# A two-layer decoder trunk: two single products of the attention branch become one seven-product pair

## The chip, the cores and the metric

The kernel runs on one core of a Trainium2 chip. The metric is the device time of one execution in microseconds (us). The time of the kernel before is 2420.99 us, the median of three runs (2418.62 to 2423.28).

## What is computed

The trunk has two layers over 256 positions of width 2048, in fp32. The part that matters here:

```python
for l in range(DEPTH):                                   # 2 layers
    h = rms_norm(x, mix_norm[l])
    q, k, v, uv, gate_logits = split(h @ w_in[l])        # 2048 x 7680
    branch_a = sliding_window_attention(q, k, v, sinks[l]) @ w_attn_branch[l]   # 1024 x 2048
    branch_b = chunked_sgu(gelu(uv), ...) @ w_sgu_branch[l]                      # 1024 x 2048
    gates = sigmoid(gate_logits)                         # two gates per channel
    merged = gates[..., :2048] * branch_a + gates[..., 2048:] * branch_b
    x = x + merged @ w_out[l]
    h2 = rms_norm(x, ffn_norm[l])
    x = x + (silu(h2 @ w_gate[l]) * (h2 @ w_up[l])) @ w_down[l]
```

The change touches one product only, `branch_a`: the attention output (256 x 1024) times `w_attn_branch[l]` (1024 x 2048).

## The kernel before

**Chunks and halves.** Each weight matrix is cut into chunks of 512 columns, and each chunk into "halves" of 256 rows, held as a tile of 128 partitions x 2 x 512. A half comes from HBM as one load of 512 KB (for `w_attn_branch` as two loads of 256 KB each, 64 partitions apiece, `rows_of`, L129). The 256 positions are two row tiles of 128.

**Three matmuls for one.** To keep fp32 accuracy every operand is split into a high part and a rest (`hi` and `lo` for weights, `uh` and `ul` for activations). For a weight half, ScalarE (ACT) writes `whi` (L261) and VectorE (DVE) writes `wlo` = raw - whi (L262). `add_product` (L353) then issues six matmuls of 128x512: for each of the two 128-row blocks uh*hi, uh*lo, ul*hi. These six are called *one product* here. The tiles `whi` and `wlo` have four buffers, so that the split of one entry cannot start before the matmuls of the entry four places earlier are done.

**Single and pair.** `single` (L125) multiplies one chunk: each half is one entry with two products, one for each row tile. `pair` (L137) takes two chunks with the same activations. For one unit (512 rows of each chunk, four halves k11, k12, k21, k22) it uses a scheme with seven block products in place of eight (entries P1 to P7, one product each); the remaining halves are ordinary entries, G for the first chunk and U for the second. The seven products need differences of the weights, made on DVE in place in the loaded tiles (`add`, L242, L246): P5 takes k12 - k11, P6 takes k22 less that, P7 takes k22 - k12, and P4 takes k21 less what P6 took. P3 multiplies k22 itself. The sums of the activations (`sh`, `sl`) already exist for the first unit. Sums that both chunks share go through a tile `kept`: after P5, ACT copies two accumulators (L384, L385); after P6 and again after P7, DVE adds the accumulator a[1] into `kept` (L387), and since P6, P7 and P4 all accumulate in a[1], P7 must not start before the L387 that follows P6 has read it. Later ACT copies `kept` into the accumulators of the second chunk (L390).

**Order.** `plans` (L172 to L196) lists the products of a layer, and `entries` is one list of all halves in order. When a pair comes, its six head entries are woven into the last entries of the plan ahead of it (L198 to L216): with six or nine of them when that plan is long, and otherwise with four. In the variant with four entries behind a pair (L211) P6, P2 and P7 stand one behind the other. PE follows this list. The order on DVE, ACT, POOL and SP is made by a scheduler at build time.

**Loads.** All weight loads are issued on the SP queue, up to seven entries ahead (`W_LOAD`). Ordinary halves rotate through five buffers. The four tiles k11, k12, k21 and k22 have one buffer each, shared by all pairs: a pair's k22 can be loaded only when the k22 of the pair ahead has been split for its P3. The k22 load stands behind other transfers in SP's order, among them the gathers of a transpose (L437: 16 transfers of 32 KB, `tt<-box`), which wait for DVE's block transposes (L431).

**Around the change.** The attention branch comes after the projection pair of gate chunks 3 and 4, and before the projection pair of gate chunks 5 and 6. Its first two chunks are a pair already. The third and fourth were two singles of four entries each. After each chunk DVE multiplies it with the gate (`gated`, L1034, L1037).

In what follows A is the pair of attention chunks 0 and 1, B the third and fourth chunk when they are a pair, and C the projection pair of gate chunks 5 and 6. "A's U" and so on name entries of that pair.

Of the kernel before, what the change touches and what calls it, by code (L numbers as in the profile page):

```python
# [28 lines left out]
NCH = D // CW  # L29
# [34 lines left out]
def hybrid_trunk(ctx: ExitStack, tc: tile.TileContext, x, mix_norm, w_in, q_norm, k_norm, sinks,  # L64
# [31 lines left out]
    def cols_of(w_ap, n):  # L96
        return [w_ap[:, j * CW:(j + 1) * CW] for j in range(n)]
# [19 lines left out]
    def load_of(w, h, tag="raw"):  # L117
        raw_no[0] += 1
        return raw_no[0], w, h, tag

    def half(w, h, tag):
        ld = load_of(w, h)
        return dict(tag=tag, h=h, loads=[ld], src=ld[0])

    def single(key, w):  # L125

        return Plan(key, [], [half(w, h, "X") for h in range(w.shape[0] // (2 * P))])
# [9 lines left out]
    def pair(key, wa, wb, by_unit=False, last_later=False, two=False):  # L137

        head, p3 = [], []
        both = (WINO, WINO + 1) if two else (WINO,)
        for w in both:
            h1, h2 = 2 * w, 2 * w + 1
            l11, l12, l21, l22 = (load_of(m, h, t if w == WINO else "slot")
                                  for m, h, t in ((wa, h1, "k11"), (wb, h1, "k12"), (wa, h2, "k21"), (wb, h2, "k22")))
            k11, k12, k21, k22 = l11[0], l12[0], l21[0], l22[0]
            head.append([dict(tag="P1", loads=[l11, l12], src=k11),
                         dict(tag="P5", loads=[], sums=[(k11, k12, k11)], src=k11),  # L150
                         dict(tag="P2", loads=[l21, l22], src=k21),
                         dict(tag="P6", loads=[], sums=[(k11, k22, k11)], src=k11),
                         dict(tag="P7", loads=[], sums=[(k12, k22, k12)], src=k12),
                         dict(tag="P4", loads=[], sums=[(k21, k21, k11)], src=k21)])
            p3.append(dict(tag="P3", loads=[], src=k22))
            for e in head[-1] + p3[-1:]:
                e["unit"], e["done"] = w, w == both[-1]
        head = [e for es in zip(*head) for e in es]
        rest = [h for h in range(wa.shape[0] // (2 * P)) if h // 2 not in both]
        g, u = [half(wa, h, "G") for h in rest], [half(wb, h, "U") for h in rest]  # L160
        body = g[:3] + p3 + g[3:] + u
        g[1]["then"] = "open"
        if last_later:
            body = g[:2] + p3 + u[:2] + g[2:] + u[2:]
        if by_unit:
            body = g[:2] + p3 + u[:2]
            g[0]["then"] = g[1].pop("then")
            for i in range(2, len(rest), 2):
                body += g[i:i + 2] + u[i:i + 2]
        return Plan(key, head, body)  # L170

    plans, by_heads = [], []  # L172
    for l in range(DEPTH):
        wl = w_in[l]

        def of_in(kind, c):
            o = {"kv": O_KV, "q": 0, "v": O_V, "u": O_U, "gate": O_GATE}[kind] + c * CW
            return wl[:, o:o + CW]

        for f in FIRST_PART[l]:  # L180
            plans.append((single if len(f) == 1 else pair)(("in", l), *(of_in(*c) for c in f)))
        by_heads += cols_of(w_attn_branch[l], NCH)
        c_ = by_heads[-NCH:]
        plans += [pair(("att", l), c_[0], c_[1])] + [single(("att", l), w) for w in c_[2:]]
        plans[-3].first = True
        c_ = cols_of(w_sgu_branch[l], NCH)
        plans += [pair(("in", l), of_in("gate", 5), of_in("gate", 6)), pair(("sgu", l), c_[0], c_[1]),
                  single(("in", l), of_in("gate", 7)), single(("sgu", l), c_[2]), single(("sgu", l), c_[3])]
        c_ = cols_of(w_out[l], NCH)
        plans += [pair(("mix", l), c_[j], c_[j + 1], last_later=j == 0) for j in range(0, NCH, 2)]  # L190
        for r, (f0, f1) in enumerate(ROUNDS):
            for f in range(f0, f1):
                plans.append(pair(("ffn", l), w_gate[l, :, f * CW:(f + 1) * CW], w_up[l, :, f * CW:(f + 1) * CW], f == 0,
                                  two=(r, f - f0) in FFN_TWO))
            c_ = cols_of(w_down[l, f0 * CW:f1 * CW, :], NCH)
            plans += [pair(("hid", l, r), c_[j], c_[j + 1], j == 0, two=(l, r, j) in HID_TWO) for j in range(0, NCH, 2)]  # L196
# [85 lines left out]
    def tick():  # L282
        slot_no[0] += 1
        due = [s for s in steps if s[0] <= slot_no[0]]
        steps[:] = [s for s in steps if s[0] > slot_no[0]]
        for _, fn in sorted(due, key=lambda s: s[0]):
            with tc.issue_after(stream.last.ins):
                fn()
# [75 lines left out]
    def step():  # L364
        e = entries[stream.at]
        p, tag = e["plan"], e["tag"]
        units = units_at[p.key]
        w = stream.next()
        if tag in "XGU":
            ps = banks(p, "b" if tag == "U" else "a")  # L370
            todo = [(ps[t], block(units, e["h"], t)) for t in range(NT)]
        else:
            which, t, form = {"P1": ("a", 1, (0, 0)), "P2": ("a", 0, (1, 0)), "P6": ("a", 1, 1), "P7": ("a", 1, 2),
                              "P4": ("a", 1, (1, 1)), "P5": ("a", 0, 0), "P3": ("b", 0, 3)}[tag]
            todo = [(banks(p, which)[t], tuple(x[:, form] for x in units[e["unit"]][2:]) if isinstance(form, int)
                     else block(units, 2 * e["unit"] + form[0], form[1]))]
        for ps, u in todo:
            add_product(p, ps, u, w, tag in ("P4", "P7"))
        a, b = p.acc.get("a"), p.acc.get("b")
        if not e.get("done", True):  # L380
            pass
        elif tag == "P5":
            p.kept = slot([P, 2, CW], name="kept")
            nc.scalar.activation(p.kept[:, 1, :], a[0], AF.Copy)  # L384
            nc.scalar.activation(a[0], a[1], AF.Copy)  # L385
        elif tag in ("P6", "P7"):
            nc.vector.tensor_tensor(out=p.kept[:, int(tag == "P7"), :], in0=a[1], in1=p.kept[:, 1, :], op=ALU.add)  # L387
        if "then" in e:
            for t, ps in enumerate(banks(p, "b")):
                nc.scalar.activation(ps, p.kept[:, t, :], AF.Copy)  # L390
                p.opened.add(id(ps))
        p.left -= 1
        if e is getattr(p, "last_g", None):
            p.calls[0](a)
        if p.left == 0 and p.paired:
            p.calls[1](b)
        debt[0] += len(todo)
        if debt[0] >= 2:
            debt[0] -= 2
            if p.left or p.paired:  # L400
                tick()

    def run(key):
        p = plans[turn_of[0]]
        turn_of[0] += 1
        assert p.key == key
        return p

    def product(key):

        p = run(key)
        while p.left:
            step()
        return p.acc["a"]

    def product_pair(key, on_a, on_b):


        p = run(key)
        p.calls = (on_a, on_b)  # L420
        while p.left:
            step()
# [575 lines left out]
    for l in range(DEPTH):  # L998

        gates = {}  # L1000
        att, spa = Attention(layer[l]), Spatial(layer[l], norm)
# [32 lines left out]
        def gated(j, ps):  # L1034
            ga = gates[j]
            for t in range(NT):
                nc.vector.scalar_tensor_tensor(out=ga[:, t, :], in0=ga[:, t, :], scalar=1.0, in1=ps[t],  # L1037
                                               op0=ALU.add, op1=ALU.mult)

        product_pair(("att", l), lambda ps: gated(0, ps), lambda ps: gated(1, ps))  # L1040
        for j in range(2, NCH):
            gated(j, product(("att", l)))
            tick()
        mT = units_at["mix", l] = [None] * NCH
        nxt = Norm(ffn_cols(l))
        units_at["ffn", l] = nxt.units
# [93 lines left out]
```

## Time and profile before

| | |
|---|---|
| time, median of 3 runs | 2420.99 us |
| time, lowest and highest | 2418.62, 2423.28 us |
| span of the profiled execution | 2416.4 us |
| median less this span | 4.6 us |
| PE, matmuls | 2405.1 us busy, 10692 instructions |
| PEld, weight loads of PE | 1970.7 us busy, 82% of the span |
| DVE | 2092.0 us busy, 87% |
| ACT | 1532.4 us busy, 63% |
| POOL | 303.4 us busy, 13% |
| granted TensorE clock | 1.000 |

The profiled execution is known by its span alone, from its first instruction to its last; what its own run took is not listed beside it, so the span is set against the median of the other runs. Matmuls are pipelined, and their ends are modelled: a row's duration overlaps the next row's start. The stretch of attention chunks 2 and 3 lies at about 311 to 333 us in the first layer and 1512 to 1534 us in the second; times in the two layers are 1201.1 us apart.

### The profile page before, as it was taken

Reading aid. Unit: us, or ns where it says so; the run is one execution under the profiler, and the core shown is the slowest. Engines: PE = TensorE matmul, PEld = TensorE weight load, DVE = VectorE, ACT = ScalarE, POOL = GpSimd, SP = SyncE. Lnnn points to the kernel's source line nnn. Section 1 sums busy time; section 2 is a strip of 40 time slices with the busy share of each in tenths; the row PEclk is TensorE's granted clock in tenths of the full one; section 3 lists DMA queues with packets and bytes.
Section 4 is the critical chain, followed back from the end, with each engine's and each line's share of the span. In section 5 each row is a group of like instructions: output and inputs, shape, how many; then the busy total and the mean of one; then the engine's idle time right before and its main releaser. Section 6 shows DMA issues by size and latency. Waiting matters only on the chain.

```text
span 2416.4 us, 31069 instructions
## 1 busy us (share of the span) xinstructions
PE 2405.1 (100%) x10692; PEld 1970.7 (82%) x10692; DVE 2092.0 (87%) x2409; ACT 1532.4 (63%) x1932; POOL 303.4 (13%) x557
## 2 busy tenths in 40 slices
PE   9999999999999999999999999999999999999999
PEld 7877888888888888888888778888888888888887
DVE  7779787898999998799887897878889989998998
ACT  6477555576666675666665775555676666666665
POOL 1100001132110111001301000011311101110010
PEclk9999999999999999999999999999999999999999
DMA  8755678687677757776957557776867786677773
GB/s 287 233 167 164 178 204 251 221 264 239 191 238 228 239 179 223 245 225 178 293 177 260 174 160 197 215 223 227 269 219 232 213 258 204 199 231 229 235 223 138
DMA packets 285070, 527.16 MB, mean 218 GB/s; under 512 B 28208, under 2 KB 40080, under 8 KB 284912
## 3 DMA queue, kind: packets, MB, share of 16 engines
q1 hardware_dynamic: 263056, 486.36, 63.6%
q0 software_dynamic: 21536, 38.56, 6.2%
q8 instruction: 83, 1.36, 0.2%
q14 instruction: 75, 0.61, 0.1%
q10 hardware_dynamic: 320, 0.27, 0.0%
HBM read 483.66 MB, written 16.78 MB: 207 GB/s over the span
## 4 chain that ended last, share of the span: by engine, by line
PE 88%; DVE 4%; DMA 4%; issue 1%; ACT 1%; SPq 1%; POOL 0%; DVEq 0%; ACTq 0%
PE acc L361 58%; PE acc L362 29%; DVE wlo L262 2%; DMA raw<-in_w_up_dram 2%; DMA raw<-in_w_in_dram 1%; DMA tt<-box 1%; ACT whi L261 1%; DVE raw L246 1%; SPq L437 1%; PE psc L807 1%; PE po L859 0%; PE psg L942 0%; PE ppt L844 0%; PE pt L474 0%; POOL tt L437 0%
## 5 line engine op out<-in xcount | busy, mean ns | idle before, releaser
L261 ACT ACTIVATE whi<-raw 128x1024 fp32r<-128x1024 f32 (+1 forms) x1116 | 1166.6, 1058 | 786.3 <-PE acc L362 440.0
L262 DVE TENSOR_TENSOR wlo<-raw,whi 128x1024 fp32r<-128x1024 f32 (+1 forms) x1117 | 1343.5, 1216 | 269.3 <-ACT whi L261 255.3
L361 PE MATMUL acc<-whi,uh 128*128 128x512 f32 x2854 | 1116.7, 391 | 1.4 <-ACT uh L460 1.4
L361 PE MATMUL acc<-wlo,uh 128*128 128x512 f32 x2854 | 1113.3, 390 | 2.1 <-DVE wlo L262 1.3
L362 PE MATMUL acc<-whi,ul 128*128 128x512 f32 x2854 | 1112.1, 390 | 0.6 <-DVE ul L465 0.6
L361 PEld LDWEIGHTS acc<-wlo,uh 128*128 128x128 f32 x2854 | 536.0, 188 | 118.5 <-DVE wlo L262 6.6
L361 PEld LDWEIGHTS acc<-whi,uh 128*128 128x128 f32 x2854 | 535.9, 188 | 117.8 <-issue 4.9
L362 PEld LDWEIGHTS acc<-whi,ul 128*128 128x128 f32 x2854 | 535.9, 188 | 112.8 <-DVE ul L465 1.5
L437 POOL DMA_DIRECT2D tt<-box x464 | 228.0, 499 | 1202.6 <-DVE box L431 339.7
L246 DVE TENSOR_TENSOR raw<-raw,raw 128x1024 f32<-128x1024 f32 x292 | 355.5, 1218 | 5.2 <-DMA raw<-in_w_up_dram 2.9
L361 PE MATMUL acc<-wlo,sh 128*128 128x512 f32 x584 | 228.1, 391 | 2.0 <-DVE wlo L262 2.0
L361 PE MATMUL acc<-whi,sh 128*128 128x512 f32 x584 | 228.4, 391 | 0.0
L362 PE MATMUL acc<-whi,sl 128*128 128x512 f32 x584 | 227.5, 390 | 0.0
L361 PEld LDWEIGHTS acc<-wlo,sh 128*128 128x128 f32 x584 | 109.7, 188 | 26.3 <-DVE wlo L262 4.1
L361 PEld LDWEIGHTS acc<-whi,sh 128*128 128x128 f32 x584 | 109.7, 188 | 25.1 <-issue 2.3
L362 PEld LDWEIGHTS acc<-whi,sl 128*128 128x128 f32 x584 | 109.6, 188 | 22.7
L387 DVE TENSOR_TENSOR kept<-acc,kept 128x512 f32<-128x512 f32 x102 | 69.6, 682 | 9.3 <-PE acc L362 9.3
L390 ACT ACTIVATE acc<-kept 128x512 f32<-128x512 f32 x102 | 59.7, 588 | 2.3 <-DVE kept L387 1.0
L964 POOL DMA_DIRECT2D held_x<-part x16 | 13.9, 868 | 301.4 <-ACT part L963 301.4
L333 POOL TENSOR_TENSOR rv<-ve,neg_half 128x4 f32<-128x4 f32 x8 | 10.2, 1273 | 266.8 <-DVE ve L907 247.9
L384 ACT ACTIVATE kept<-acc 128x512 f32<-128x512 f32 x51 | 30.1, 591 | 10.8 <-PE acc L362 10.5
L829 ACT ACTIVATE pr<-pr,negm 128x128 f32<-128x128 f32 x64 | 24.9, 390 | 16.0 <-DVE negm L820 16.0
(149 smaller groups left out, 909.0 us busy)
## 6 DMA issues: line engine op xcount, KB each, us to landing
raw<-in_w_in_dram SPq DMA_DIRECT2D x239, 512.0 KB, 4.8
raw<-in_w_gate_dram SPq DMA_DIRECT2D x176, 512.0 KB, 4.6
raw<-in_w_up_dram SPq DMA_DIRECT2D x176, 512.0 KB, 5.4
raw<-in_w_down_dram SPq DMA_DIRECT2D x176, 512.0 KB, 5.3
raw<-in_w_out_dram SPq DMA_DIRECT2D x64, 512.0 KB, 6.9
raw<-in_w_attn_branch_dram SPq DMA_DIRECT2D x64, 256.0 KB, 7.0
raw<-in_w_sgu_branch_dram SPq DMA_DIRECT2D x32, 512.0 KB, 5.8
tt<-box POOLq DMA_DIRECT2D x464, 32.0 KB, 4.7
```

The costliest lines, as they stand in the source:

```text
L246: self.last = nc.vector.tensor_tensor(out=self.raws[d], in0=self.raws[x], in1=self.raws[y], op=ALU.subtract)
L261: self.high = nc.scalar.activation(hi[:, i, :], raw[:, i, :], AF.Copy)
L262: self.last = nc.vector.tensor_tensor(out=lo[:, i, :], in0=raw[:, i, :], in1=hi[:, i, :].bitcast(F32), op=ALU.subtract)
L361: nc.tensor.matmul(ps, a, part[:, kk, :], start=first and kk + n == 0, stop=False, skip_group_check=True)
L362: nc.tensor.matmul(ps, b, hi[:, kk, :], start=False, stop=kk == 1, skip_group_check=True)
L384: nc.scalar.activation(p.kept[:, 1, :], a[0], AF.Copy)
L387: nc.vector.tensor_tensor(out=p.kept[:, int(tag == "P7"), :], in0=a[1], in1=p.kept[:, 1, :], op=ALU.add)
L390: nc.scalar.activation(ps, p.kept[:, t, :], AF.Copy)
L437: q.dma_start(dst[j * B:(j + 1) * B, i], box[i * B:(i + 1) * B, j])
L807: nc.tensor.matmul(pscore[:, i, :nk], self.qT[pair // 4][j * HD:(j + 1) * HD, pair % 4, t * P:(t + 1) * P], self.kT[j * HD:(j + 1) * HD, : ...
L829: self.exps = nc.scalar.activation(pr4[:, h, :], pr4[:, h, :], AF.Exp, bias=nm_[:, h:h + 1], accum_out=den[:, h:h + 1])
L964: nc.gpsimd.dma_start(held_x[j], part, accum_op=ALU.add)
```

## The change

Chunks 2 and 3 of the attention branch become a second `pair` in place of two `single` plans. The mark `first` (which keeps a pair's first accumulators in the pool `ps_acc`) stays with pair A, which is now two places from the end of the list and not three. Pair B takes its first accumulators from the pool `ps_at`. The loop at the end calls `product_pair` twice.

```diff
         c_ = by_heads[-NCH:]
-        plans += [pair(("att", l), c_[0], c_[1])] + [single(("att", l), w) for w in c_[2:]]
-        plans[-3].first = True
+        plans += [pair(("att", l), c_[j], c_[j + 1]) for j in range(0, NCH, 2)]
+        plans[-2].first = True
...
-        product_pair(("att", l), lambda ps: gated(0, ps), lambda ps: gated(1, ps))
-        for j in range(2, NCH):
-            gated(j, product(("att", l)))
-            tick()
+        for j in range(0, NCH, 2):
+            product_pair(("att", l), lambda ps, j=j: gated(j, ps), lambda ps, j=j: gated(j + 1, ps))
```

Line numbers behind this place are two lower in the changed kernel. The order of entries on PE becomes: A's P4, G0, G1 | B's P1, A's P3, B's P5, A's U0, B's P6, P2, P7, A's U1, B's P4 | B's G0, G1, C's P1, B's P3, C's P5, B's U0, C's P6, P2, P7, B's U1, C's P4. C's head was woven into the last single before, in the other variant with four entries.

First place: DVE in the first layer, from the split of A's G1 on. Before:

```order
L262 TENSOR_TENSOR wlo_2784<-raw_2737,whi_2783 128x1024
L262 TENSOR_TENSOR wlo_2806<-raw_2595,whi_2805 128x1024
L262 TENSOR_TENSOR wlo_2819<-raw_2766,whi_2818 128x1024
L262 TENSOR_TENSOR wlo_2838<-raw_2780,whi_2837 128x1024
L1037 SCALAR_TENSOR_TENSOR gate_1055<-gate_1055,acc_2643 128x512
L1037 SCALAR_TENSOR_TENSOR gate_1055<-gate_1055,acc_2644 128x512
L262 TENSOR_TENSOR wlo_2863<-raw_2802,whi_2862 128x1024
L262 TENSOR_TENSOR wlo_2877<-raw_2815,whi_2876 128x1024
```

raw_2595 is A's k22, raw_2766 and raw_2780 are A's U0 and U1, and the last two rows are halves of the third chunk. The same place now, where raw_2750 and raw_2753 are B's k11 and k12, raw_2805 its k21, raw_2808 its k22, and raw_2802 A's U0:

```order
L262 TENSOR_TENSOR wlo_2823<-raw_2595,whi_2822 128x1024
L1037 SCALAR_TENSOR_TENSOR gate_1055<-gate_1055,acc_2643 128x512
L262 TENSOR_TENSOR wlo_2839<-raw_2750,whi_2838 128x1024
L1037 SCALAR_TENSOR_TENSOR gate_1055<-gate_1055,acc_2644 128x512
L262 TENSOR_TENSOR wlo_2862<-raw_2802,whi_2861 128x1024
L246 TENSOR_TENSOR raw_2750<-raw_2808,raw_2750 128x1024
L262 TENSOR_TENSOR wlo_2877<-raw_2750,whi_2876 128x1024
L246 TENSOR_TENSOR raw_2753<-raw_2808,raw_2753 128x1024
L262 TENSOR_TENSOR wlo_2888<-raw_2805,whi_2887 128x1024
L262 TENSOR_TENSOR wlo_2904<-raw_2753,whi_2903 128x1024
L246 TENSOR_TENSOR raw_2805<-raw_2805,raw_2750 128x1024
L387 TENSOR_TENSOR kept_2897<-acc_2866,kept_2897 128x512
```

Ahead of the first of these rows stand now, behind A's G1, the split of B's P1 and the difference k12 - k11. The difference with raw_2808 stands four rows behind the split of raw_2595, which used the same buffer, and the L387 of P6 stands behind the split of P7 and the difference for P4.

Second place: SP in the second layer, around the 16 gathers of the SGU transpose. Before, raw_13283 being C's k22:

```order
L235 DMA raw_13281<-in_w_in_dram 128x2x512
L235 DMA raw_13162<-in_w_attn_branch_dram 64x2x512 x2
L235 DMA raw_13181<-in_w_attn_branch_dram 64x2x512 x2
L235 DMA raw_13283<-in_w_in_dram 128x2x512
L235 DMA raw_13206<-in_w_attn_branch_dram 64x2x512 x2
```

And now, raw_13368 being C's k22 and raw_13366 its k21:

```order
L235 DMA raw_13366<-in_w_in_dram 128x2x512
L235 DMA raw_13481<-in_w_in_dram 128x2x512
L235 DMA raw_13494<-in_w_in_dram 128x2x512
L437 DMA tt_13325<-box_13326 32x256 x16
L235 DMA raw_13368<-in_w_in_dram 128x2x512
L235 DMA raw_13524<-in_w_in_dram 128x2x512
```

C's k22 stood eight places ahead of the gathers; now it stands directly behind them. In the first layer it stands directly ahead of them.

## The prediction, on record before the result

> **What bounds the kernel now.** I read the page first, then the groups, then the two stretches of the change in time.
>
> ```profile
> span 2416.4 us, 31069 instructions
> PE 2405.1 (100%) x10692; PEld 1970.7 (82%) x10692; DVE 2092.0 (87%) x2409; ACT 1532.4 (63%) x1932; POOL 303.4 (13%) x557
> PE 88%; DVE 4%; DMA 4%; issue 1%; ACT 1%; SPq 1%; POOL 0%; DVEq 0%; ACTq 0%
> ...
> L361 PE MATMUL acc<-whi,uh 128*128 128x512 f32 x2854 | 1116.7, 391 | 1.4 <-ACT uh L460 1.4
> L262 DVE TENSOR_TENSOR wlo<-raw,whi 128x1024 fp32r<-128x1024 f32 (+1 forms) x1117 | 1343.5, 1216 | 269.3 <-ACT whi L261 255.3
> L246 DVE TENSOR_TENSOR raw<-raw,raw 128x1024 f32<-128x1024 f32 x292 | 355.5, 1218 | 5.2 <-DMA raw<-in_w_up_dram 2.9
> ```
>
> PE never rests for long: span less busy is 11.3 us, and the chain of waits is 88% PE. So a matmul taken away shortens the run by its place in the row of matmuls, and any new wait of PE lengthens it by its full length. DVE is 87% busy, so there is little to hide a wait behind. The stretches in question, first layer (us from the span's start; columns PE, PEld, DVE, ACT, POOL, clock, DMA share, GB/s):
>
> ```profile
> 300.00:320.00 20.00, 20.00 (x90) 16.57 (x89) 13.53 (x14) 10.46 (x12) 0.00 (x0) 1.00 1.04 236
> 320.00:340.00 20.00, 20.00 (x90) 16.58 (x89) 17.84 (x19) 13.37 (x17) 0.00 (x0) 1.00 0.56 158
> ```
>
> PE is full in both, DVE has 6.5 us free in the first (the singles) and 2.2 us in the second, and the DMA engines are saturated at 236 GB/s in the first, because loads run seven entries ahead.
>
> **The gain.** A row's 391 ns is not what a matmul costs, since rows overlap. Starts (column 1) tell:
>
> ```profile
> 300.85 0.39 PE L361 MATMUL acc<-wlo,uh 128*128 128x512 f32 x1
> ...
> 302.21 0.39 PE L361 MATMUL acc<-whi,uh 128*128 128x512 f32 x1
> ...
> 303.57 0.39 PE L361 MATMUL acc<-whi,uh 128*128 128x512 f32 x1
> ```
>
> 302.21 is the first matmul of A's G0 (A's P4, which takes `wlo` first, began at 300.85); 1.36 us are six matmuls, one product, so 0.227 us each. Two singles are 2 x 4 x 2 = 16 products; the pair is 7 + 4 x 2 = 15. One product a layer goes: 2 x 1.36 = **-2.7 us** (-0.11%). By the 391 ns it would be -4.7 us.
>
> **What is added on DVE and ACT.** The pair splits 11 tiles where the singles split 8. Per layer DVE gets 3 splits, 4 differences (L246) and 2 `kept` (L387); ACT 3 splits and 4 half-size copies. Back to back, starts lie closer than the busy times:
>
> ```profile
> 287.67 1.23 DVE L262 TENSOR_TENSOR wlo<-raw,whi 128x1024 fp32r<-128x1024 f32 x1 [0.57 <-ACT whi L261]
> 288.81 1.22 DVE L246 TENSOR_TENSOR raw<-raw,raw 128x1024 f32<-128x1024 f32 x1
> ...
> 294.90 0.68 DVE L387 TENSOR_TENSOR kept<-acc,kept 128x512 f32<-128x512 f32 x1
> 295.50 2.35 DVE L262 TENSOR_TENSOR wlo<-raw,whi 128x1024 fp32r<-128x1024 f32 x2
> ```
>
> 1.14 us for a full tile, 0.60 for a half: 7 x 1.14 + 2 x 0.60 = 9.2 us of DVE a layer, ACT 3 x 1.06 + 4 x 0.59 = 5.5 us (ACT is under 70% there and pays nothing). From B's P1 to C's P4 PE has 26 products = 35.4 us; DVE has 20 splits, 8 differences, 4 `kept`, 6 gate products and 2 transposes, 28 x 1.14 + 12 x 0.60 = 39.1 us. So DVE alone is 3.7 us short. Splits lead PE by three entries (4.1 to 8.2 us), so the price of this alone lies between 0 and 3.7 us a layer; I take it as contained in the chain that follows, which is longer.
>
> **The wait that I expect: k22.** B's k22 uses the buffer of A's k22, and is free when A's P3 is split. Before, C had this place in the row, but used its tile only at 325.69. What the trace of before shows of that moment:
>
> ```profile
> 301.63 1.05 ACT L261 ACTIVATE whi<-raw 128x1024 fp32r<-128x1024 f32 x1
> 302.72 1.23 DVE L262 TENSOR_TENSOR wlo<-raw,whi 128x1024 fp32r<-128x1024 f32 x1 [1.65 <-ACT whi L261]
> 303.97 0.37 SPq L235 DMA_DIRECT2D raw<-in_w_in_dram  x1
> 301.74 0.60 SPq L235 DMA_DIRECT2D raw<-in_w_attn_branch_dram  x1
> 325.69 1.22 DVE L246 TENSOR_TENSOR raw<-raw,raw 128x1024 f32<-128x1024 f32 x1
> ```
>
> ACT's and DVE's rows are A's P3; 0.02 us after it SP issues the next k22. Now B's P1 and the difference for P5 stand in front of P3: +2 x 1.14, so k22 is issued at 306.3, its second part at 306.9. When does it land? SP's row 301.74 is the last load ahead of it in the same place of the queue. Issue to landing of single loads, in the order of issue at 293.87, 301.74 and 303.97, then the attention load of the second layer issued at 1502.83, then all attention loads:
>
> ```profile
> raw<-in_w_in_dram SPq DMA_DIRECT2D x1, 512.0 KB, 4.4
> raw<-in_w_attn_branch_dram SPq DMA_DIRECT2D x1, 256.0 KB, 9.1
> raw<-in_w_in_dram SPq DMA_DIRECT2D x1, 512.0 KB, 9.5
> raw<-in_w_attn_branch_dram SPq DMA_DIRECT2D x1, 256.0 KB, 7.8
> DMA to landing us min/median/max: 3.9/7.0/9.7
> ```
>
> Behind an idle DMA a load takes 4.4 us, behind the backlog 9. The load of 301.74 lands at 310.8; 512 KB more at 236 GB/s take 2.2: **k22 lands at 313.0** in the first layer. In the second, 1502.83 + 7.8 + 2.2 = 1512.8, less 1201.1: 311.7.
>
> From there the chain is serial, because each step waits for the one before: difference 1.22, `whi` 1.06, `wlo` 1.14 to the next start (P6), difference k22 - k12 1.14, `wlo` of P2 1.14, `wlo` of P7 1.14, difference for P4 1.14, `kept` of P6 0.68; with 0.3 for the hand-overs 9.0 us. Then P7 may overwrite a[1]. On schedule P7 starts 11 products after 302.21, at 317.17. It can start at 313.0 + 9.0 = 322.0: **4.8 us late**, and in the second layer 311.7 + 9.0 = 320.7: **3.5 us**. Bounds: with the least landing, 3.9, 306.9 + 3.9 + 9.0 = 319.8, 2.6 us; with 9.5, 8.2 us. What is late next are all later products, and the time is lost, since PE has no idle time to win back.
>
> Of what stands behind this stalled difference on DVE, A's U1 and B's P4 and G0 are ready before PE asks. Not so **C's k22**, which waits for B's P3. First layer: after `kept` at 322.0, DVE does three splits (325.4), then `kept`, gate, split, transpose, gate, split and the split of P3: 3 x 1.14 + 4 x 0.60 + 0.1 = 5.9, so k22 is issued at 331.3. Six 512 KB loads go out ahead of it from about 321 on; at 2.2 us each behind a first of 4.4 it lands six us after issue, 337.3. Here `kept` of P6 stands ahead of P7's split, and the chain to P7 is 7.7: 345.0. P7 is due at 337.57 + 4.8 = 342.4: 2.6 late, and 0.7 more for the split of B's U1, which comes behind: **3.3 us** (1.7 with a landing of 4.4, 6.8 with 9.5).
>
> Second layer: the load stands behind 16 gathers on SP. What these cost in the trace of before:
>
> ```profile
> 1502.73 1.05 ACT L261 ACTIVATE whi<-raw 128x1024 fp32r<-128x1024 f32 x1
> 1523.69 0.70 DVE L431 STREAM_TRANSPOSE box<-u 128x512 f32<-128x512 f32 x1
> 1524.61 10.08 SPq L437 DMA_DIRECT2D tt<-box  x16
> 1534.79 1.05 SPq L235 DMA_DIRECT2D raw<-in_w_in_dram  x2
> ```
>
> (1502.73 is the 301.63 of this layer.) They start when the second transpose ends and hold SP for 10.1 us; the next load goes out right behind. Now, in the first layer's clock: `kept` ends at 320.7, three splits 324.1, transpose, `kept`, gate, split, transpose 3.7: 327.8; gathers until 337.9; k22 lands 4.4 later at 342.3, and with the long chain P7 starts at 351.3. Due is 337.57 + 3.5 = 341.1: **10.2 us late**. This hangs least on the landing: 9.7 at 3.9 us, 15.3 at 9.5.
>
> **Sum.** 4.8 + 3.3 + 3.5 + 10.2 - 2.7 = +19.1 us; 2416.4 + 19.1 = 2435.5 of span, and with the 4.6 us between the span and the median of the runs, **2440 us** (+0.8%). The scheduler also moves a few rows on DVE, ACT and SP behind the change; all of PE's waits in the trace together are 11.3 us, so I allow 4 us either way for it.
>
> The Trainium skill ("DMA: Bandwidth & Descriptors", section Anatomy of one DMA) gives about 2.0 us fixed plus bytes over 436 GB/s for a transfer, fitted to another issue path; an estimate by it is 2.6 us for 256 KB, and the late starts would then be 1.3, 0.7, 1.3 and 9.0, the sum +9.6 and the time 2431. The trace has 3.9 at the least and 9 behind a backlog, so it does not bear the rule out here.
>
> **The rivals.**
> - *The loads meet an idle queue* (3.9 to 4.4 us): 2.6 + 1.7 + 2.6 + 10.2 - 2.7 = +14.4, 2435 us. For it: B needs no load more than the singles did. Against it: 236 GB/s in 300 to 320. The skill's rule above goes this way, and further than any row.
> - *The gathers don't hold C's k22 in the second layer*, since they were 0.2 us ahead of DVE's need before: then it costs 3.3 as in the first, +12.2, 2433 us. Against it: SP is in order, and the row 1534.79 starts when the gathers end.
> - *The loads come in time, DVE is the bound*: 2 x 3.7 - 2.7 = +4.7, 2426 us (+0.2%). For it: 39.1 against 35.4 us. Against it: DVE gets to the difference with k22 when A's U0 is split, whose `whi` waits for A's G1 (307.65 + 0.2 + 1.06 + 1.14 = 310.1); k22 would have to land by then, 3.2 us after its second part is issued.
> - *Not slower: the lead covers it all.* Splits run three entries ahead, and P7 is on time if k22 lands by 317.17 - 9.0 = 308.2. That is the point from which it decides. Then only the product counts: 2421.0 - 2.7 = 2418.3. For it: PE takes `whi` first in P6 and P2, so parts of the chain overlap with matmuls. Against it: no load of the trace lands within the 1.9 us from the issue, and DVE is not there before 310.1.
>
> **How the numbers follow.** Chances: forecast 0.58 (its tail of landings at 9.5, 8.2 + 6.8 + 8.2 + 15.3 - 2.7 = +35.8 or 2457, in it with 0.05), idle queue 0.10, gathers 0.12, DVE bound 0.12, covered 0.08. A measurement of this kernel tells about 0.2% from no change: 2416.2 to 2425.8. The covered case is "same" but for 0.03 (if the other rows move well too); the DVE case lies on the edge, half of it "same": same 0.12, faster 0.03, slower 0.85. Range 2427 to 2453: it leaves out the covered and the DVE case and the far tail, 0.2 together.
>
> **What would show it.** PE's busy time falls by 12 matmuls, yet the span grows. PE's waits name DVE `kept` L387 and `wlo` L262, DVE's L246 waits for `raw<-in_w_attn_branch_dram` (first B) and `in_w_in_dram` (C) for several us each, in the second layer most, right behind the 16 gathers. C's k22 is issued at the end of the gathers in the second layer and ahead of them in the first. I am wrong if L246 finds its k22 landed in these four places, if P7 follows P2 without a gap, or if the gain shows as -2.7 us.

## The result: 1.6% slower, twice the forecast loss

The changed kernel takes **2458.4 us** (median of 4 runs, 2457.8 to 2460.1), beside 2420.5 us for the kernel before on the same chip: the ratio is 1.0159, with a 95% interval of 1.0145 to 1.0173. The forecast was 2440, with a range of 2427 to 2453. The direction was right and the size was not: +38 us instead of +19.

From the page of the changed kernel, its busy times, and from the groups two that grew:

```profile
span 2456.1 us, 31083 instructions
PE 2417.1 (98%) x10680; PEld 1974.3 (80%) x10680; DVE 2111.1 (86%) x2427; ACT 1544.7 (63%) x1946; POOL 302.7 (12%) x557
...
L361 PE MATMUL acc<-whi,sh 128*128 128x512 f32 x600 | 237.9, 397 | 24.7 <-ACT acc L385 19.1 <-ACT whi L261 5.6
L246 DVE TENSOR_TENSOR raw<-raw,raw 128x1024 f32<-128x1024 f32 x300 | 366.1, 1221 | 20.6 <-DMA raw<-in_w_attn_branch_dram 7.1 <-DMA raw<-in_w_in_dram 6.6 <-DMA raw<-in_w_up_dram 4.1
```

PE has 12 matmuls less, and its busy time has grown by 12 us all the same: some matmuls run at half clock (below), and the last one ahead of a gap counts with its full length. Matmuls with the sums as stationary operand (`whi,sh`, in P3, P5, P6 and P7 of a pair) now wait 24.7 us, 19.1 of them for the copy L385. The differences L246 wait 13.7 us for the attention and projection weights, where before they waited only for other weights and 5.2 us in all.

**Where the time went.** With PE never resting, it issues a matmul every 0.227 us, so the matmuls missing from a stretch of given length tell the loss there. The same four stretches in the kernel before (columns PE, PEld, DVE, ACT, POOL, clock, DMA share, GB/s):

```profile
300.00:400.00 100.00, 100.00 (x443) 82.84 (x442) 81.42 (x86) 59.89 (x69) 1.68 (x4) 1.00 0.75 220
400.00:1480.00 1080.00, 1078.48 (x4796) 882.11 (x4795) 942.06 (x1091) 693.67 (x885) 156.60 (x282) 1.00 0.71 220
1480.00:1640.00 160.00, 160.00 (x708) 132.51 (x707) 127.46 (x136) 93.85 (x108) 11.84 (x24) 1.00 0.71 205
1640.00:2400.00 760.00, 757.85 (x3344) 625.64 (x3343) 697.23 (x710) 495.42 (x574) 109.99 (x214) 1.00 0.71 226
```

And in the changed kernel:

```profile
300.00:400.00 100.00, 93.98 (x402) 75.87 (x401) 82.42 (x86) 60.53 (x72) 0.00 (x0) 0.98 0.69 208
400.00:1480.00 1080.00, 1065.26 (x4720) 870.97 (x4719) 932.23 (x1076) 688.09 (x876) 157.31 (x285) 1.00 0.70 217
1480.00:1640.00 160.00, 150.65 (x639) 121.90 (x638) 125.91 (x135) 88.24 (x102) 2.44 (x5) 0.97 0.66 190
1640.00:2400.00 760.00, 758.59 (x3346) 625.69 (x3345) 687.95 (x704) 492.09 (x572) 119.71 (x234) 1.00 0.73 228
```

41, 76, 69 and -2 matmuls are missing: 9.3 us in the stretch of the change in the first layer, 17.3 us in the rest of that layer, 15.7 us in the second layer's stretch, -0.5 behind it. Their sum, less the 2.7 us of the two products, is 39.1 us; the span grew by 39.7. The two stretches together lose 25.0 us, where the prediction had 21.8. **The rest of layer 1 loses 17.3 us, for which the prediction had nothing but its 4 us for moved rows.**

**The stretch in the first layer.** DVE in the changed kernel, three single rows:

```profile
313.33 1.23 DVE L246 TENSOR_TENSOR raw<-raw,raw 128x1024 f32<-128x1024 f32 x1 [4.07 <-DMA raw<-in_w_attn_branch_dram]
...
321.52 0.69 DVE L387 TENSOR_TENSOR kept<-acc,kept 128x512 f32<-128x512 f32 x1
...
336.65 1.23 DVE L246 TENSOR_TENSOR raw<-raw,raw 128x1024 f32<-128x1024 f32 x1
```

B's difference with k22 waits 4.07 us for the load and starts at 313.33 (forecast 313.0), and the L387 that lets P7 go ends at 322.2 (forecast 322.0). But C's difference with k22, at 336.65, has no wait in brackets: it follows straight on DVE's own work. C's k22 was there, though only just: it was issued at 331.43 and landed at 336.56.

PE at the same place, around P6:

```profile
313.31 0.39 PE L362 MATMUL acc<-whi,ul 128*128 128x512 f32 x1
317.82 0.73 PE L361 MATMUL acc<-whi,sh 128*128 128x512 f32 x1 [4.12 <-ACT acc L385]
318.35 0.63 PE L361 MATMUL acc<-wlo,sh 128*128 128x512 f32 x1
318.78 0.63 PE L362 MATMUL acc<-whi,sl 128*128 128x512 f32 x1
...
322.27 0.49 PE L361 MATMUL acc<-wlo,sh 128*128 128x512 f32 x1
```

PE stands before P6 from 313.31 to 317.82, a gap that the prediction put before P7. Then starts lie 0.43 us apart instead of 0.227: the granted clock is halved for a while. P7 starts at 322.27, right behind L387, so here the slow matmuls only filled time in which P7 could not start anyway. A's G0 starts at 301.30 in this execution and P7 comes 66 matmuls behind it, so P7 was due at 316.27: it is 6.0 us late.

**The stretch in the second layer.** SP, and below it DVE:

```profile
1545.58 8.43 SPq L235 DMA_DIRECT2D raw<-in_w_in_dram  x6
1554.30 10.07 SPq L437 DMA_DIRECT2D tt<-box  x16
1564.47 1.04 SPq L235 DMA_DIRECT2D raw<-in_w_in_dram  x2
```

```profile
1538.41 1.23 DVE L246 TENSOR_TENSOR raw<-raw,raw 128x1024 f32<-128x1024 f32 x1 [3.01 <-DMA raw<-in_w_attn_branch_dram]
...
1568.70 1.23 DVE L246 TENSOR_TENSOR raw<-raw,raw 128x1024 f32<-128x1024 f32 x1 [6.64 <-DMA raw<-in_w_in_dram]
```

The first pair of waits is as forecast: B's k22 late, then C's k22 right behind the 16 gathers, landing 4.1 us after its issue.

### The profile page after: what moved, and what is told of

Same layout as the page of the kernel before. It is cut to its first block, busy times and chain, and to the rows that moved or that the text cites. A ratio compares the mean times of both kernels' runs of the same rounds, so it can differ in the third digit from the quotient of the medians.

```text
span 2456.1 us, 31083 instructions
## 1 busy us (share of the span) xinstructions
PE 2417.1 (98%) x10680; PEld 1974.3 (80%) x10680; DVE 2111.1 (86%) x2427; ACT 1544.7 (63%) x1946; POOL 302.7 (12%) x557
## 4 chain that ended last, share of the span: by engine, by line
PE 87%; DVE 4%; DMA 4%; issue 2%; ACT 2%; SPq 1%; POOL 0%; DVEq 0%; ACTq 0%; POOLq 0%
PE acc L361 57%; PE acc L362 28%; DVE wlo L262 2%; DMA raw<-in_w_in_dram 2%; ACT whi L261 1%; SPq L437 1%; DVE raw L246 1%; DMA tt<-box 1%; PE psc L807 1%; PE po L859 0%; DMA raw<-in_w_attn_branch_dram 0%; DMA raw<-in_w_gate_dram 0%; PE psg L942 0%; PE ppt L844 0%; DMA raw<-in_w_up_dram 0%
## 5 line engine op out<-in xcount | busy, mean ns | idle before, releaser
L246 DVE TENSOR_TENSOR raw<-raw,raw 128x1024 f32<-128x1024 f32 x300 | 366.1, 1221 | 20.6 <-DMA raw<-in_w_attn_branch_dram 7.1
L361 PE MATMUL acc<-whi,sh 128*128 128x512 f32 x600 | 237.9, 397 | 24.7 <-ACT acc L385 19.1
L361 PE MATMUL acc<-wlo,sh 128*128 128x512 f32 x600 | 237.7, 396 | 4.1 <-DVE wlo L262 3.9
L362 PE MATMUL acc<-whi,sl 128*128 128x512 f32 x600 | 236.4, 394 | 0.0
L387 DVE TENSOR_TENSOR kept<-acc,kept 128x512 f32<-128x512 f32 x106 | 72.7, 686 | 9.2 <-PE acc L362 9.2
L384 ACT ACTIVATE kept<-acc 128x512 f32<-128x512 f32 x53 | 31.3, 590 | 16.1 <-PE acc L362 15.7
L1074 ACT ACTIVATE hid<-acc,rstd 128x512 f32<-128x512 f32 x44 | 28.7, 682 | 10.0 <-PE acc L362 10.0
```

The costliest lines, as they stand in the source:

```text
L246: self.last = nc.vector.tensor_tensor(out=self.raws[d], in0=self.raws[x], in1=self.raws[y], op=ALU.subtract)
L361: nc.tensor.matmul(ps, a, part[:, kk, :], start=first and kk + n == 0, stop=False, skip_group_check=True)
L362: nc.tensor.matmul(ps, b, hi[:, kk, :], start=False, stop=kk == 1, skip_group_check=True)
L1074: nc.scalar.activation(hid[:, t, :], g[t], AF.Silu, scale=norm.r[t])
```

## The experiments

All times are medians on the device; ratios are to the kernel before, timed on the same chip. On the chips used, the kernel before took 2418.2 to 2420.5 us, so times of two rows compare to about 2 us. Losses are the matmuls missing against the kernel before in the four stretches above, times 0.227 us:

| kernel | time, us | ratio (95%) | span | 300–400 | 400–1480 | 1480–1640 | 1640–2400 |
|---|---|---|---|---|---|---|---|
| changed | 2458.4 | 1.0159 (1.0145–1.0173) | 2456.1 | 9.3 | 17.3 | 15.7 | -0.5 |
| `e1_count` | 2434.1 | 1.0062 (1.0049–1.0076) | 2431.5 | 9.8 | -1.4 | 9.3 | 0.7 |
| `e2_flip` | 2438.9 | 1.0083 (1.0067–1.0098) | 2436.6 | 0 | 20.0 | 0 | 0.7 |
| `e3_own22` | 2444.5 | 1.0105 (1.0091–1.0119) | 2442.8 | 5.0 | 19.5 | 3.9 | 0.7 |
| `e4_own22_count` | 2423.8 | 1.0018 (1.0009–1.0027) | 2420.9 | 4.8 | -0.7 | 4.1 | 0.2 |
| `e5_lean` | 2419.3 | 1.0004 (0.9995–1.0013) | 2417.5 | 2.7 | -0.5 | 1.6 | 0.7 |
| `e6_pool` | 2436.7 | 1.0077 (1.0065–1.0089) | 2434.2 | 9.5 | 1.1 | 10.2 | 0.2 |
| `e7_gather` | 2450.8 | 1.0135 (1.0122–1.0148) | 2448.7 | 8.9 | 16.1 | 8.2 | 1.4 |
| `e8_flip2` | 2444.2 | 1.0103 (1.0086–1.0120) | 2441.0 | 0 | -0.7 | 1.1 | 25.0 |

**The suspect for the rest of layer 1.** Other work (gate sums, norms, transposes, GELU) is not put into the program where it is written, but in *slots*. `step`, which does one entry, counts its products (one in the head of a pair, else two) and fires a slot after every two (L397 in the changed kernel, and the lines behind it); `tick` then issues what is due behind the latest split:

```python
debt[0] += len(todo)
if debt[0] >= 2:
    debt[0] -= 2
    if p.left or p.paired:
        tick()
```

Two singles are 16 products, 8 slots (the last one of each fired by the loop that the change removed). The pair is 15: 7 slots and one product left over. From there on all slots fire one product later than in the kernel before, until the second layer's pair leaves another one over and they fire where they did before. The diff does not show this. Theory **S**: this shift costs the 17 us. Rival **R**: the later losses are an after-effect of the late loads, whatever the slots.

### `e1_count`: the changed kernel, count made good

```diff
         for j in range(0, NCH, 2):
             product_pair(("att", l), ...)
+        debt[0] += 1
+        if debt[0] >= 2:
+            debt[0] -= 2
+            tick()
```

> The changed kernel, with pair B counted as 16 products and not 15 in the count that fires the slots of the helper work, so that all work behind the attention branch is again ordered as in the kernel before; pair B, its loads and its waits stay. Theory S (the 17 us that the changed kernel loses between 400 and 1000 us come from slots that fire half a step off, which moves DVE and ACT rows at pairs far behind): these gaps go and the time is about 2442 us. Rival R (they are after-effects of the late k22, loads and DVE knocked out of step): the time stays at 2458 us, since k22 is as late as before.

2434.1 us, 24.3 us less than the changed kernel. The rest of layer 1 loses nothing any more:

```profile
400.00:1480.00 1080.00, 1078.89 (x4802) 883.67 (x4801) 944.70 (x1096) 694.54 (x884) 158.34 (x285) 1.00 0.70 221
1480.00:1640.00 160.00, 155.02 (x667) 126.51 (x666) 127.44 (x135) 93.16 (x109) 11.85 (x24) 0.98 0.69 200
```

More went than S expected, because the second layer's stretch gained 6.4 us too. SP tells why:

```profile
1527.79 11.61 SPq L235 DMA_DIRECT2D raw<-in_w_in_dram  x7
1540.82 10.08 SPq L437 DMA_DIRECT2D tt<-box  x16
1550.99 0.53 SPq L235 DMA_DIRECT2D raw<-in_w_in_dram  x1
```

Seven projection loads, C's k22 the last of them, go out ahead of the gathers, where the changed kernel sent six. So the shift, carried over from layer 1, had also put the gathers ahead of C's k22 in layer 2.

### `e2_flip`: the kernel before, counted as 15

The two singles stay, with all their loads and no second pair; only the slot behind the fourth chunk is counted as half:

```diff
         for j in range(2, NCH):
             gated(j, product(("att", l)))
-            tick()
+            debt[0] += 2 if j == 2 else 1
+            if debt[0] >= 2:
+                debt[0] -= 2
+                tick()
```

> The kernel before, with its two single chunks, but its slot count moved half a step as the changed kernel has it behind the attention branch; no pair B. Theory S: slower than before by about 16 us, 2436 us, with gaps of PE ahead of P6 at about 440, 530 and 890 us. Rival R: the time of before, 2420.5 us, since no k22 is late.

2438.9 us, about 20 us above the kernel before on its chip (ratio 1.0083), with no pair B and no late k22. The loss is all in the rest of layer 1 (20.0 us). R falls. The waits of PE, and one of the gaps:

```profile
PE acc L361 <- ACT acc L385: 11.9, 3, 5.5
```

```profile
439.09 0.39 PE L362 MATMUL acc<-whi,ul 128*128 128x512 f32 x1
443.56 0.79 PE L361 MATMUL acc<-whi,sh 128*128 128x512 f32 x1 [4.08 <-ACT acc L385]
```

The changed kernel has the same gap, 4.46 us from 446.70 to 451.16 with the same 4.08 us behind L385, and the same of 2.68 and 5.91 us later on.

What happens in these gaps is seen on ACT. The last of them, at 911 to 917 us in the changed kernel:

```profile
909.77 2.01 ACT L261 ACTIVATE whi<-raw 128x1024 fp32r<-128x1024 f32 x2 [1.21 <-DVE raw L246]
911.68 1.04 ACT L505 ACTIVATE sh<-sums 128x1024 fp32r<-128x1024 f32 x1
912.63 1.04 ACT L261 ACTIVATE whi<-raw 128x1024 fp32r<-128x1024 f32 x1
913.58 0.57 ACT L384 ACTIVATE kept<-acc 128x512 f32<-128x512 f32 x1
914.05 1.25 ACT L1074 ACTIVATE hid<-acc,rstd 128x512 f32<-128x512 f32 x2
915.20 1.15 ACT L456 ACTIVATE uh<-tt 128x512 fp32r<-128x512 f32 x2
916.24 0.60 ACT L385 ACTIVATE acc<-acc 128x512 f32<-128x512 f32 x1
```

The same place in the kernel before:

```profile
889.81 0.60 ACT L384 ACTIVATE kept<-acc 128x512 f32<-128x512 f32 x1 [0.66 <-PE acc L362]
890.44 0.58 ACT L385 ACTIVATE acc<-acc 128x512 f32<-128x512 f32 x1
```

P6 may start when L385 has copied P5's accumulator. Before, L384 and L385 follow one another as soon as PE is done with P5. With the slots shifted, steps of a slot (L1074 and L456, 2.2 us) stand between them, and L384 itself comes late, since ACT has been busy without a pause from 909.77. So L385 starts 5.3 us after the start of PE's last matmul ahead of P6, at 910.97.

The first gap comes about in another way. ACT in the changed kernel, before PE goes on at 451.16 (in `e2_flip` the same rows, with the same wait, begin at 441.35):

```profile
448.95 1.06 ACT L261 ACTIVATE whi<-raw 128x1024 fp32r<-128x1024 f32 x1 [3.84 <-DVE raw L246]
449.92 0.58 ACT L384 ACTIVATE kept<-acc 128x512 f32<-128x512 f32 x1
450.53 0.58 ACT L385 ACTIVATE acc<-acc 128x512 f32<-128x512 f32 x1
```

And the same copies in the kernel before:

```profile
437.05 0.60 ACT L384 ACTIVATE kept<-acc 128x512 f32<-128x512 f32 x1 [0.24 <-PE acc L362]
437.54 1.05 ACT L261 ACTIVATE whi<-raw 128x1024 fp32r<-128x1024 f32 x1
438.49 0.59 ACT L385 ACTIVATE acc<-acc 128x512 f32<-128x512 f32 x1
```

Here no step of a slot stands between the copies. They stand behind a split for which ACT waits 3.84 us, until DVE has made the difference, and ACT is idle meanwhile. What the gaps share is that the shift changed the order of rows made at build time, and that L384 and L385 came to stand behind rows that are ready later. Why the scheduler orders them so stays open.

### `e8_flip2`: the same count in the second layer only

If the shift itself is what costs, the rest of layer 2 must pay for it as well once the slots are off there.

```diff
-            debt[0] += 2 if j == 2 else 1
+            debt[0] += 2 if j == 2 and l == 1 else 1
```

> The kernel before with its two single chunks, counted as 15 products in place of 16 in the second layer only, so that everything up to there is the kernel before, and the slots behind fire half a step off to the end. In the changed kernel, and in the kernel before counted as 15 in both layers, the second count puts the slots right again for the rest of layer 2, and that rest lost only 1 to 2 us. Theory S (slots off by half a step are what costs): layer 2 behind the attention branch now loses what layer 1 lost there, some 10 to 20 us, with waits of P6 for the copy L385 as in layer 1: 2430 to 2440 us. Theory L (something of layer 1 alone, such as its loads or its order of rows, makes it costly): layer 2 loses 0 to 3 us, 2418 to 2424 us.

2444.2 us: +24.5. The 400 to 1480 stretch is that of the kernel before, and the rest of layer 2 loses 25.0 us:

```profile
1640.00:2400.00 760.00, 742.84 (x3234) 610.89 (x3235) 674.16 (x686) 480.89 (x559) 109.60 (x214) 0.99 0.71 222
```

```profile
1639.36 0.39 PE L362 MATMUL acc<-whi,ul 128*128 128x512 f32 x1
1643.82 0.50 PE L361 MATMUL acc<-whi,sh 128*128 128x512 f32 x1 [4.08 <-ACT acc L385]
```

The first gap is that of layer 1, 4.46 us with the same 4.08 us for L385; those of 2.68 and 5.89 us follow (at 1730.6 and 2104.9), and one of 3.18 at 2181.1 that layer 1 did not have. S holds, and what was left of the idea that something of layer 1 alone is to blame falls. S explains too why the changed kernel lost nothing behind the second stretch: there the slots fire where they did before.

### `e3_own22` and `e4_own22_count`: k22 in a tile of its own

What remains in the stretches is the k22 chain. Theory K: the shared buffer of k22 is all of it. Theory D: DVE is short of time there in any case. B's k22 goes to a tile of the large pool `big` (31 buffers), not to the one that A's k22 holds:

```diff
-            l11, l12, l21, l22 = (load_of(m, h, t if w == WINO else "slot")
+            l11, l12, l21, l22 = (load_of(m, h, t if w == WINO and t not in own else "slot")
...
-        plans += [pair(("att", l), c_[j], c_[j + 1]) for j in range(0, NCH, 2)]
+        plans += [pair(("att", l), c_[j], c_[j + 1], own=("k22",) if j else ()) for j in range(0, NCH, 2)]
```

> The changed kernel, with pair B's k22 loaded into a tile of the large pool and not into the one k22 buffer, so that it need not wait for A's P3, nor C's k22 for B's P3; the slot count is as in the changed kernel. Theory K (the 22 us in the two attention stretches are the late k22, with the clock that drops after a gap): the gaps there go, DVE's L246 waits for no load, about 2437 us. Rival D (DVE has too much work there, the load only hides it): some 4 us a layer stay, about 2445 us. Rival R (the later gaps hang on the late k22 too): about 2420 us.

> Both edits, k22 of pair B in its own tile and the slot count as before. Theories S and K together: only the two products less are left, 2418 us, 0.1% under before. With rival D: 2423 to 2427 us. With rival R: as the run with the own k22 alone.

2444.5 us, and with the count made good as in `e1_count` 2423.8 us. In the first, the stretches lose 5.0 and 3.9 us, not 9.3 and 15.7; the rest of layer 1 still loses 19.5, as S has it and R does not. The two edits together form a square:

| | count 15 | count 16 |
|---|---|---|
| k22 in the shared buffer | 2458.4 | 2434.1 |
| k22 in its own tile | 2444.5 | 2423.8 |

The count is worth 24 or 21 us, the buffer 14 or 10. With both mended the kernel is still 0.18% slower than before. The stretches of that version:

```profile
300.00:400.00 100.00, 97.07 (x422) 78.38 (x421) 86.77 (x91) 62.83 (x74) 0.00 (x0) 1.00 0.72 215
1480.00:1640.00 160.00, 157.69 (x690) 128.93 (x689) 133.69 (x142) 96.17 (x112) 11.81 (x24) 1.00 0.70 204
```

They lose 4.8 and 4.1 us, 8.9 in all: near the 2 x 3.7 that the prediction gave as the price of DVE alone, and more than the 2.7 us gained. K falls as the whole cause, and what is left has D's size. C's part of it is not the load: C's k22, no longer held up by B's, lands 16 us ahead of its difference here, and PE's four gaps at C's head in the first layer are those of the changed kernel (0.97, 1.00, 0.68 and 0.78 us). For B, DVE's row of the difference shows that the load is not quite hidden either:

```profile
308.93 1.23 DVE L246 TENSOR_TENSOR raw<-raw,raw 128x1024 f32<-128x1024 f32 x1 [0.85 <-DMA raw<-in_w_attn_branch_dram]
```

### `e5_lean`: less for DVE

To test D, four differences a layer (P5 and P4 of B and of C) are left out of that version; those products take the undiminished tiles, so what is computed there is not the reference.

```diff
+            for e in (head[-1][1], head[-1][5]) if lean else ():
+                e["sums"] = []
```

> The version with its own tile for k22 and the count made good (2423.8 us), but in B and C the differences of P5 and P4 are left out (four DVE rows of 1.14 us a layer; these products then take the tiles as they are, so that the output is another). In the version with them PE's starts lose 4.6 us in the first stretch and 3.7 in the second. Theory D (DVE has more to do there than PE, 39.1 against 35.4 us, and that is all that is left): 4.56 us less a layer is more than the shortage, the losses go and the product's gain shows, 2416 to 2418 us. Theory H (what is left is the chain of hand-overs from DVE to ACT to PE behind each difference, whatever DVE's load): the two differences in the chain to P6 are still there, at most half of the loss goes, 2420 to 2424 us.

2419.3 us (a ratio of 1.0004, no difference from before), a little above D's numbers and below H's. The losses fall from 8.9 to 4.3 us: half goes. Which half can be seen. In the first layer the gaps of C (four between 0.68 and 1.01 us in the version with the differences) are gone but for one of 0.68 us, so there it was DVE's load. B's gap before P7 stays (1.39, now 1.24 us), with another of 1.16 us shortly ahead of it, and so does the cause on DVE:

```profile
309.16 1.23 DVE L248 TENSOR_TENSOR raw<-raw,raw 128x1024 f32<-128x1024 f32 x1 [1.83 <-DMA raw<-in_w_attn_branch_dram]
```

Even in its own tile k22 lands only just before 309.2, behind a full queue of loads, and the prediction's point for P7 being on time was 308.2. Neither theory holds alone. By the gaps, DVE's load makes about half and the chain from k22 about half; no run has the chain alone taken away.

### `e6_pool`: the same four differences on POOL

Everything is computed again, and DVE is relieved, which would beat both kernels if POOL did the work for nothing.

```diff
-                        self.last = nc.vector.tensor_tensor(...)
+                        on = nc.gpsimd if "on_pool" in entries[self.summed] else nc.vector
+                        made = on.tensor_tensor(...)
```

> The same version with everything computed, but the differences of P5 and P4 in B and C run on POOL, not on DVE. No run here has such a row on POOL. If it takes no more than 3 us there and leaves DVE alone, D expects most of what leaving them out brings: 2416 to 2420 us, at or a little below before (2420.5). If it takes 4 us or more, or holds DVE's rows up while it runs, P5 and P4 wait for it: 2425 to 2440 us. H expects 2422 to 2426 us with a fast POOL.

2436.7 us, about 13 us above the version with all differences on DVE. POOL's row and the DVE row beside it:

```profile
303.41 2.39 POOL L249 TENSOR_TENSOR raw<-raw,raw 128x1024 f32<-128x1024 f32 x1 [69.96 <-DVE wlo L266]
```

```profile
303.57 3.32 DVE L266 TENSOR_TENSOR wlo<-raw,whi 128x1024 fp32r<-128x1024 f32 x1 [0.24 <-ACT whi L265]
```

POOL takes 2.39 us, which is under the 3 us set for it, but the DVE row beside it takes 3.32 instead of 1.22 and ends at 306.89, 1.1 us after POOL's. DVE did not run until POOL was done. So DVE loses 2.1 us where it saves 1.1, and where POOL's other difference falls together with P7's split, PE waits for that `wlo` (four gaps of 2.5 us). No version run here beats the kernel before.

### `e7_gather`: the gathers off SP

The changed kernel, with the gathers of the second branch issued by POOL:

```diff
-                after(U_TURN[i], lambda i=i, ut=ut: transposed(self.sguT, i, ut, queue=nc.sync,
+                after(U_TURN[i], lambda i=i, ut=ut: transposed(self.sguT, i, ut, queue=nc.gpsimd,
```

> The changed kernel (2458.4 us), with the 16 gathers of each chunk of the second branch issued by POOL in place of SP, in both layers. Theory G (the gathers on SP hold C's k22 back in the second layer): the wait of L246 for in_w_in (6.64 us) goes, PE's gap of 5.6 us there goes with its half clock, and the second stretch loses about 9 us like that of the version with the count made good, not 15.6: 2452 us (2449 to 2454); the layer behind the first stretch stays as slow as it is. Theory N (k22 would have been late anyway): 2457 to 2460 us.

2450.8 us. The span is 7.4 us shorter than that of the changed kernel, by 7.5 us less loss in the second stretch (8.2 instead of 15.7), and no difference of C waits for its load any more. Theory G holds. The first layer is as slow as it was.

## Why the prediction was right and wrong

**Right.** That the pair is slower, and the places. Each term of the sum, against the starts of PE in the changed kernel. Measured is what P7 loses against matmuls 0.227 us apart from the first gap on, and in brackets the gaps of that place, start to start:

| term | forecast | measured |
|---|---|---|
| B, layer 1 | 4.8 | 6.0 (gaps of 4.51 and 0.53) |
| C, layer 1 | 3.3 | 2.3, and 0.8 behind P7 (0.97, 1.01, 0.70, 0.79) |
| B, layer 2 | 3.5 | 5.0, and 0.7 behind P7 (3.46, 0.63) |
| C, layer 2 | 10.2 | 9.1, and 0.7 behind P7 (5.60, 1.26, 0.59, 0.79, 0.59) |

The chain is as it was worked out. B's k22 landed at 313.2 for 313.0, and L387 ended 9.0 us behind it, at 322.2, as forecast. B's terms come out larger for two small reasons: in the first layer PE is 0.9 us ahead of the earlier profile in this execution, and in the second DVE takes up k22 6.8 us after its issue (1531.60 to 1538.41) where the forecast had it land after 5.4. Behind the gathers, 10.2 us were 9.1, and taking the gathers away gave 7.5 us of that stretch back. B's k22 landed about 7 us after the issue that was worked out for it, so the rival "idle queue" falls. The transfer time of the Trainium skill ("DMA: Bandwidth & Descriptors", Anatomy of one DMA), 2.6 us for 256 KB by an estimate, does not agree with these 7 us either.

**Wrong, the step that failed.** "The scheduler also moves a few rows on DVE, ACT and SP behind the change; all of PE's waits in the trace together are 11.3 us, so I allow 4 us either way for it." The present waits of PE say nothing about what other rows would cost. The rows did not move at a scheduler's whim: the scheduler got another program, since 15 products in place of 16 shift every slot behind the pair by one product, in all of layer 1. That cost 17.3 us there, and in `e2_flip` 20.0 us by itself, without any other part of the change. The number 15 stands in the prediction, as a gain; that the program counts products to place its other work was not asked.

**Wrong in mechanism, near in size.** C's term in layer 1 was put down to its k22 landing late. Nothing waits for that load: DVE reaches the difference late because it is behind with its own work. It was close, since k22 landed 0.1 us before the difference, but with the load 16 us early (`e4_own22_count`) the gaps are the same. That is the third rival's mechanism ("DVE is the bound"), and with the other two causes mended (`e4_own22_count`) it gives 2423.8 us, where the rival said 2426. In the same way "the gathers don't hold C's k22" came true in `e1_count`: their place depended on the slots.

**Not foreseen, and small.** The half clock after a stall. In the two stretches it cost next to nothing: its spells behind the three long gaps lie ahead of a P7 that L387 released, so PE would have waited instead. In the rest of layer 1 no such wait follows, and 18 starts at half clock make 3.6 us by an estimate (0.20 us each), part of the 17.3. PE's busy time grew by 12.0 us, for the slow rows and the rows ahead of gaps, where the prediction had it fall by 12 matmuls. The -2.7 us of the gain could not be seen alone in any run; that the spans agree with the losses less 2.7 us within 1.3 us in all of these runs that have the pair is the only sign of it.

**Two slips in the working.** Seven loads from 321 us, 4.4 us for the first and 2.2 for each other, end at 338.6, not at the 337.3 that was used for C's k22 (it landed at 336.56). And the chances that the range leaves out, 0.08, 0.12 and 0.05, make 0.25, not 0.2.

## What to carry to other kernels

When a program places its side work by counting steps, a change in the count is a change of its own: look for the counter, restore it, and time that first, or the verdict is on the shift and not on the edit. A tile with a single buffer costs by the distance of its uses, so when a new user comes between two old ones, follow the load from the release to the first use, through the queue that it stands in. And a saving on the engine that is the bound is only worth having if its neighbour has the time: here 1.4 us of matmuls a layer were paid with 9.2 us of work on an engine that was 87% busy.

## What the runs showed of the hardware

**A short stall halves the clock for a while.** In the ten traces, once PE is under way, all 16 gaps of PE of 3.46 us or more (start to start) are followed by 6 to 13 matmuls that start 0.43 us apart. Of the 12 gaps between 2.2 and 3.3 us, 7 are; a gap of 2.68 us is in three traces and is not in two. Single gaps under 2.2 us never are. In the clock's own records each spell is 3.41 or 6.83 us at 0.5. At 0.20 us each the slow starts cost 1.2 to 2.6 us on top of the stall, where nothing else hides it. The Trainium skill ("TensorE: Matmul & The Clock Gate", Part 1) describes a half-rate state set by a free-running activity window of about 3.4 us, which agrees with the spells and with their dependence on chance. The Trainium skill (the same page, "Why this matters for your kernels") asks for no gaps above about 3 us. Here 2.68 us were enough three times, and 2.2 us once, with a gap of 0.75 us shortly ahead of it.

**POOL and DVE exclude each other on such rows.** A subtraction of 128x1024 fp32 takes 2.39 us on POOL and 1.22 on DVE. In all eight places of `e6_pool` a DVE subtraction that meets it takes 3.02 to 3.36 us and ends about 1.1 us after POOL's, so it starts in effect when POOL's ends. The Trainium skill ("SBUF — State Buffer", Who interferes with whom) states this as an exclusive lock on a shared port pair; the trace agrees.
